# Query projection with the weights held still and rotated along partitions, and one fixed instruction order for a whole two-layer backbone

## The chip, the cores and the metric

The kernel runs on one core of a Trainium2 chip. It is one launch that holds a whole network of two layers. Its time is device microseconds (us), the median of several executions; the profile is of one execution and counts from the first to the last instruction (the span). Engines are named as in the profile: PE (TensorE matmul) with PEld (its weight load), DVE (VectorE), ACT (ScalarE), POOL (GpSimd), and SP, which here only issues transfers. A matmul holds a tile of 128x128 (its "weights") in the array and streams the columns of the other operand past it: "128x512" in a row of the profile is an output of 128 partitions and 512 columns.

## What is computed

Latents `x` (512 tokens x 1024) go through two layers. Each is a token mixer and a dense SwiGLU feed-forward network (FFN), both between RMS norms with shift, scale and gate made from a conditioning vector (`ada`). Layer 0 mixes with windowed grouped-query attention: 16 query heads of 64, 4 key/value heads, a window of 128 tokens to each side, 256 context tokens that every query sees, and a sink logit per head. Layer 1 mixes with a chunked gMLP. Cut to what the change touches:

```
def apply_rope(x, cos, sin):                       # per head of 64: two halves of 32
    x1, x2 = split(x, 2)
    return concat([x1*cos - x2*sin, x2*cos + x1*sin])

def window_sink_mixer(h_lat, h_ctx, w_qkv, w_o, sink, cos, sin):
    q, k, v = split(h_lat @ w_qkv)
    q = apply_rope(q, cos, sin) * 64**-0.5
    k = apply_rope(k, cos, sin)
    ...                                            # softmax over band, context and sink
    return o @ w_o                                 # a plain output projection

def chunk_gmlp(h, ...):
    u, v = split(gelu(h @ w_in + b_in))
    mixed = w_s · layernorm(v) + b_s
    return (u * mixed) @ w_o                       # the other plain output projection
```

## The kernel before

**Arithmetic.** Everything is 32 bits wide. For a full-rate matmul an operand is split into a high part (a cast on ACT, `high`, L217) and a low part, the rest (a subtraction on DVE, `low`, L224); a product is then three matmuls: high by high, high by low, low by high. Weights arrive from memory as `w_raw` in units of 1 MB, and are split into `w_hi` and `w_lo`.

**Stages**, by their time in the profile: norm, modulation and the key/value projection (0 to 78 us); attention (78 to 240); its output projection, called WO (240 to 300); the first FFN (300 to 600), most of it in products of half-size blocks (256 columns), seven in place of eight; the input projections of the gMLP (600 to 716); its output projection, called GO, and the head of the second FFN (716 to 790); the rest of the second FFN (to the end).

**The query path before.** There are 8 pairs `p`, each of four query heads and two tiles of 128 tokens (512 columns in PSUM). `q_project` holds a tile of the activations `HA` still and streams 256 columns of the query weights, 2 tiles x 8 slices x 3 products for a pair, so that the result has tokens on partitions. Then come `q_rows` (ACT copies it out, L736), `rotate` (two multiplications on POOL, L731, and two on DVE, L732, with the table `rope`), `q_add` (DVE, L745), `q_split` (high part on ACT, low part on DVE, L752), `q_turn` (eight PE transposes, L759, since the scores want head dimensions on partitions) and `q_copy` (two ACT copies, L760). A tile `qT` holds in its upper 64 partitions the low part of what the lower 64 hold high, so that a score needs two matmuls, one with `khi` and one with `klo`.

**Attention.** There are 16 blocks, 4 key/value groups x 4 token tiles, with four heads each. A head goes through `score` (PE, L905, into one of two `s_ps` buffers), `bound` (DVE adds the mask and takes the row's bound, L911), `exp` (ACT, L916), `normalise` (POOL, L932), `turn` (PE transposes the probabilities), `turned` (ACT or DVE copy them, L945), `value` (PE), `rows_out` and `store` (L963, L969). Pieces of the query projection of later pairs, of `ada` and of the WO projection stand between these on the same engines.

**What sets the order.** A step is a small function with a due time, `at(time, step, ...)`; `run_plan` (L604) sorts the steps collected so far and calls them. A table of names, `ORDER`, goes before the due times: a step whose name is in it takes its place in the table, and the others follow by time. Inside a "manual schedule" each engine gets its instructions in just the order in which the steps are called; outside one, the framework decides how to interleave them. Before, the table has 1575 names: the start, the attention, and the second half of each plain output projection. The FFNs and the gMLP went by their due times. The first half of each plain output projection (`down`, L1194: units 0 and 1 of four) was not made of steps: loops called `ws.unit`, `ready` (which splits the activations into `st` tiles) and `work` outside a manual schedule. In GO those loops also advanced a generator, `shift_sums` (L1945), which adds up one vector of the second FFN.

An engine works off its instructions in order; one that waits holds up those behind it. The same is true of SP's queue of transfers (`dma`, L214).

## Time and profile before

| | |
|---|---|
| time, median of 3 executions | 1109.83 us (1109.54 to 1112.11) |
| span of the profiled execution | 1108.2 us |
| time less span | 1.6 us |
| PE busy | 1088.3 us, 98% of the span |
| DVE busy | 943.8 us, 85% |
| ACT busy | 612.6 us, 55% |
| POOL busy | 255.9 us, 23% |
| granted PE clock, mean | 0.999 |

The profiled execution has no time of its own beside its span; the 1.6 us are the median less the span. In a row of grouped instructions stand the line, the engine, the operation, what is written from what, the shape, the count, then the busy time and the mean length of one in ns, then the idle time of the engine ahead of them with what ended it. In a row of stretches stand from:to, its length, and the busy time (with the number of instructions) of PE, PEld, DVE, ACT and POOL, then the granted PE clock, the busy share of the DMA engines and GB/s. In a row of waits stand the total, how often, and the longest, in us. Matmuls overlap, and their ends are modelled, so a group's mean length is longer than the pace at which matmuls follow each other; the pace is read from a stretch in which PE is busy throughout.

### The profile page before, as it was taken

The page shows a single profiled execution, that of the slowest core. Times are in us where ns is not written, and L with a number is a line of the kernel's source. Part 1 is how long each engine was busy: PE and PEld are TensorE (multiplying, and loading weights), DVE is VectorE, ACT ScalarE, POOL GpSimd, SP SyncE. Part 2 cuts the span into 40 slices and gives each one's busy share as a digit, 9 for nine tenths or more (in the row PEclk, how much of TensorE's full clock was granted, in tenths as well). Part 3 has the DMA queues.
Part 4 walks back from the last instruction along what each step waited for, and adds up shares of the span by engine and source line. Part 5 has one row for each costly group of instructions (what it writes and reads, how often), then busy time and mean ns, then how long its engine had stood idle before and what let it go on. Part 6 is the DMA issues. An engine that isn't in the chain of part 4 may idle for free.

```text
span 1108.2 us, 17883 instructions
## 1 busy us (share of the span) xinstructions
PE 1088.3 (98%) x6974; PEld 954.9 (86%) x6974; DVE 943.8 (85%) x1418; ACT 612.6 (55%) x1060; POOL 255.9 (23%) x276
## 2 busy tenths in 40 slices
PE   7999999999999999999999999999999999999997
PEld 4788877768799999998888788887999999998876
DVE  5788988958999999987988778878988888879985
ACT  6457767756555545545665534337555545546652
POOL 2517575624600000001321411006400000002300
PEclk9999999999999999999999999999999999999999
DMA  9652333243245655449964286652233343369821
GB/s 366 266 182 86 136 96 115 77 135 113 109 143 172 224 159 185 171 141 330 225 122 128 68 323 241 205 194 77 70 133 124 132 152 126 126 222 319 158 40 76
DMA packets 48857, 179.15 MB, mean 162 GB/s; under 512 B 4859, under 2 KB 9211, under 8 KB 37637
## 3 DMA queue, kind: packets, MB, share of 16 engines
q1 hardware_dynamic: 41220, 163.34, 42.3%
q0 software_dynamic: 7552, 14.68, 7.9%
q8 instruction: 54, 0.88, 0.3%
q14 instruction: 31, 0.25, 0.1%
HBM read 171.71 MB, written 2.10 MB: 157 GB/s over the span
## 4 chain that ended last, share of the span: by engine, by line
PE 64%; DVE 6%; POOL 2%; issue 2%; ACT 1%; DMA 1%; POOLq 0%; DVEq 0%; SPq 0%; ACTq 0%
PE f L1449 35%; PE y L1633 13%; PE y L1660 4%; PE v L281 4%; PE y L281 2%; PE u L1869 1%; PE u L1867 1%; PE u L1868 1%; POOL tmp L1166 1%; DVE w_lo L224 1%; DVE tmp L1170 1%; DVE x L1154 1%; PE mix L1882 1%; DMA w_raw<-in_w 1%; DVE a_sum L1378 1%
## 5 line engine op out<-in xcount | busy, mean ns | idle before, releaser
L1449 PE MATMUL f<-H,w_hi 128*128 128x256 f32 x960 | 178.6, 284 | 1.1 <-DVE fc L1460 0.5
L1449 PEld LDWEIGHTS f<-H,w_hi 128*128 128x128 f32 x960 | 149.7, 192 | 2.3 <-DVE fc L1460 1.4
L1449 PE MATMUL f<-H,w_lo 128*128 128x256 f32 x480 | 135.8, 283 | 0.0
L1633 PE MATMUL y<-w_hi,s 128*128 128x512 f32 x448 | 120.1, 389 | 0.0
L1449 PE MATMUL f<-S,w_hi 128*128 128x256 f32 x640 | 118.6, 283 | 0.0
L217 ACT CAST w_hi<-w_raw 128x1024 fp32r<-128x1024 f32 x90 | 94.5, 1053 | 39.9 <-PE y L1633 8.9
L217 ACT CAST w_hi<-T 128x1024 fp32r<-128x1024 f32 x80 | 83.7, 1047 | 52.4 <-PE f L1449 33.7
L1456 ACT COPY fc<-f 128x256 f32<-128x256 f32 x120 | 44.6, 372 | 105.8 <-PE f L1449 102.7
L224 DVE TENSOR_TENSOR w_lo<-w_raw,w_hi 128x1024 fp32r<-128x1024 f32 (+1 forms) x81 | 96.3, 1193 | 6.7 <-ACT w_hi L217 6.7
L1449 PEld LDWEIGHTS f<-S,w_hi 128*128 128x128 f32 x640 | 99.9, 192 | 0.0
L1633 PEld LDWEIGHTS y<-w_hi,s 128*128 128x128 f32 x448 | 84.1, 188 | 17.5
L224 DVE TENSOR_TENSOR w_lo<-T,w_hi 128x1024 fp32r<-128x1024 f32 x80 | 97.3, 1216 | 0.0
L1449 PEld LDWEIGHTS f<-H,w_lo 128*128 128x128 f32 x480 | 92.1, 192 | 0.0
L1449 PE MATMUL f<-S,w_lo 128*128 128x256 f32 x320 | 90.7, 284 | 0.5 <-DVE w_lo L224 0.5
L1621 POOL DMA_DIRECT2D t<-in_w x48 | 42.2, 929 | 186.5 <-PE y L1660 88.4
L383 DVE SCALAR_TENSOR_TENSOR acc<-ada_k,sc,acc 128x1024 f32<-128x1024 f32 x56 | 71.6, 1278 | 10.3 <-DMA ada_k<-in_ada 8.4
L397 POOL DMA_DIRECT2D acc<-acc x8 | 6.9, 866 | 314.2 <-DVE acc L383 310.4
L1633 PE MATMUL y<-w_lo,s 128*128 128x512 f32 x224 | 69.1, 390 | 0.6 <-DVE w_lo L224 0.6
L1449 PE MATMUL f<-H,x 128*128 128x256 f32 x480 | 64.3, 283 | 0.0
L932 POOL TENSOR_SCALAR p<-p,st 128x512 f32<-128x512 f32 (+1 forms) x64 | 53.4, 849 | 44.4 <-DVE st L928 11.7
L281 PE MATMUL y<-w_hi,st 128*128 128x512 f32 x224 | 62.3, 391 | 0.0
L1449 PEld LDWEIGHTS f<-S,w_lo 128*128 128x128 f32 x320 | 61.4, 192 | 0.9 <-DVE w_lo L224 0.9
(255 smaller groups left out, 2851.6 us busy)
## 6 DMA issues: line engine op xcount, KB each, us to landing
w_raw<-in_w SPq DMA_DIRECT2D x67, 1024.0 KB, 5.0
ada_k<-in_ada SPq DMA_DIRECT2D x56, 512.0 KB, 5.2
ada_raw<-in_ada SPq DMA_DIRECT2D x12, 1024.0 KB, 4.8
w<-in_w SPq DMA_DIRECT2D x12, 1024.0 KB
t<-in_w POOLq DMA_DIRECT2D x48, 256.0 KB, 6.1
ada<-in_ada SPq DMA_DIRECT2D x8, 1024.0 KB, 11.2
t<-in_w SPq DMA_DIRECT2D x8, 1024.0 KB, 9.2
w_raw<-in_w SPq DMA_DIRECT2D x10, 512.0 KB, 5.6
```

The costliest lines, as they stand in the source:

```text
L217: nc.scalar.copy(out=hi, in_=src)
L224: (eng or nc.vector).tensor_tensor(out=v(lo), in0=v(src), in1=v(hi).bitcast(F32), op=ALU.subtract)
L281: nc.tensor.matmul(dst, l, w[:, n * 512:(n + 1) * 512], start=first and i == 0, stop=last and i == 2)
L383: nc.vector.scalar_tensor_tensor(out=self.acc, in0=self.raws.pop(k), scalar=sc[:, k:k + 1], in1=self.acc, op0=ALU.mult, op1=ALU.add)
L932: nc.gpsimd.tensor_scalar(out=p, in0=p, scalar1=self.st[:, 12 + j:13 + j], scalar2=1.0, op0=ALU.mult, op1=ALU.mult)
L1154: nc.vector.scalar_tensor_tensor(out=xt, in0=self.tmp[:, c0:c1], scalar=self.r, in1=xt, op0=ALU.mult, op1=ALU.add)
L1166: nc.gpsimd.tensor_tensor(out=self.tmp[:, D:], in0=x[:, self.t, :], in1=self.nxt[0], op=ALU.mult)
L1449: nc.tensor.matmul(dst, l[:, w], r[:, k, :], start=first and k == 0 and j == 0, stop=k == 3 and j == 2, skip_group_check=True)
L1456: nc.scalar.copy(out=self.c[n][:, i * 256:(i + 1) * 256], in_=self.ps[n, 1 if i == 1 else 0])
L1621: nc.gpsimd.dma_start(out=self.tt[:, p * D + 512 * i:p * D + 512 * (i + 1)], in_=a["w"][F2[self.layer] + 1 + 2 * p + i][:, c:c + 512], acc ...
L1633: nc.tensor.matmul(self.bank7(i, j), st[:, c:c + P], w[:, z * 512:(z + 1) * 512], start=i == 1 and p == 0 and l == 0 and z == 0, stop=p == ...
L1660: nc.tensor.matmul(self.y[t][n], st[:, x + t * P:x + (t + 1) * P], parts[h][w][:, n * 512:(n + 1) * 512], start=v == 0 and h == 0 and i == ...
```

## The change

**Query path.** `q_project(p, k)` now holds 128 columns of the query weights still and streams all 512 tokens, so a pair is two heads for all tokens, and head dimensions come out on partitions. There are 8 pairs still; a group of four heads needs two of them. Both halves of a head are then 32 partitions apart: `q_swap` exchanges them with four transfers on SP's queue (32 partitions x 2 KB each, within SBUF). `q_rows` copies with the scale, `q_cos` and `q_add` are DVE, `q_sin` is POOL, `q_high` and `q_low` (two each, 64 partitions) write the split result straight into `q_X`. The eight transposes and two copies of a pair are gone. `q_cos` works in place, so it waits for the four transfers. The rotation table is transposed once, by 24 small matmuls (`rope_turn`), into `ropeT`. Some buffers shrink: `p` from 11 to 9, `pt` of the attention and `o_sb` from 2 to 1.

**Order.** The table has 3352 names and covers the whole program; the manual schedule stays open to the end. The first half of both plain output projections is made of steps (`stage_hi`, `stage_lo`, `work`, fetches and splits of weights), as are `shift_sums` and the transfers of `x`. With `parted=True` (GO) the steps collected so far run before the buffers are lent on (`lend_units`). A line of the new table in the attention:

```
-q_step_2_1 q_step_2_2 m4fetch_0 score_0_0 q_step_2_3 bound_0_0 exp_0_0 score_0_1 q_step_2_4 m2fetch_gain score_0_2
...
```

The table itself is left out; what it does is shown by the rows further down. The core of the diff:

```diff
-    def q_project(dst, u, t, k):
-
-        hi, lo = (p[:, (k % 4) * 256:(k % 4 + 1) * 256] for p in ws.halves[u, k // 4])
-        mm3(dst, HA[:, k, t * P:(t + 1) * P], HA[:, KC + k, t * P:(t + 1) * P], hi, lo, k == 0, k == KC - 1)
+    def q_project(p, k):
+
+        c = (k % 4) * 256 + (p % 2) * P
+        hi, lo = (w[:, c:c + P] for w in ws.halves[Q0 + p // 2, k // 4])
+        for i, (w, x) in enumerate(((hi, k), (hi, KC + k), (lo, k))):
+            nc.tensor.matmul(q_ps[p], w, HA[:, x, :], start=k == 0 and i == 0, stop=k == KC - 1 and i == 2)
...
+    def rope_turn(z):
+
+        tables[z] = ps = bankA("rope")
+        n = 32 << z
+        for t in range(NT):
+            for r in range(0, P, n):
+                nc.tensor.matmul(ps[r:r + n, t * P:(t + 1) * P], tables["k"][:, t, 32 * z:32 * z + n], ident,
+                                 start=True, stop=True, tile_position=(0, r))
...
-    def q_split(tmp):
-
-        qs = stage("qs").rearrange("p (h d) -> p h d", h=8)
-        q3 = tmp[:, 0:512].rearrange("p (h d) -> p h d", h=8)
-        nc.scalar.activation(out=qs[:, :, 0:HD], in_=q3, func=AF.Copy, scale=HD ** -0.5)
-        nc.vector.scalar_tensor_tensor(out=qs[:, :, HD:], in0=q3, scalar=HD ** -0.5,
-                                       in1=qs[:, :, 0:HD].bitcast(F32), op0=ALU.mult, op1=ALU.subtract)
-        return qs
-
-    def q_turn(qT, qs, i, bank):
-        ps = bank("qT_ps")[:, 0:512]
-        for h in range(GRP):
-            nc.tensor.transpose(ps[:, h * P:(h + 1) * P], qs[:, i * GRP + h, :].bitcast(F32), ident)
-        return lambda: nc.scalar.copy(out=qT[:, :, i * P:(i + 1) * P], in_=ps.rearrange("p (h s) -> p h s", h=GRP))
...
+    def q_rows(p):
+        q_rot[p] = vec("q_rot")
+        nc.scalar.activation(out=q_rot[p][:, 0:SEQ], in_=q_ps[p], func=AF.Copy, scale=HD ** -0.5)
+
+    def q_swap(p):
+
+        for h in range(4):
+            d = 32 * (h ^ 1)
+            dma(q_rot[p][d:d + 32, SEQ:], q_rot[p][32 * h:32 * h + 32, 0:SEQ])
+
+    def q_cos(p):
+        v = q_rot[p][:, 0:SEQ]
+        nc.vector.tensor_tensor(out=v, in0=v, in1=ropeT[:, 0:SEQ], op=ALU.mult)
+
+    def q_sin(p):
+        v = q_rot[p][:, SEQ:]
+        nc.gpsimd.tensor_tensor(out=v, in0=v, in1=ropeT[:, SEQ:], op=ALU.mult)
+
+    def q_add(p):
+        v = q_rot[p][:, 0:SEQ]
+        nc.vector.tensor_tensor(out=v, in0=v, in1=q_rot[p][:, SEQ:], op=ALU.add)
+
+    def q_high(p, z):
+
+        if z == 0:
+            q_X[p] = att_p.tile([P, 2, SEQ], F32R, name="q_X", tag="q_X", bufs=4)
+        r = slice(z * HD, (z + 1) * HD)
+        high(q_X[p][r, z, :], q_rot[p][r, 0:SEQ])
+
+    def q_low(p, z):
+        r, o = slice(z * HD, (z + 1) * HD), slice((1 - z) * HD, (2 - z) * HD)
+        low(q_X[p][o, z, :], q_X[p][r, z, :], q_rot[p][r, 0:SEQ])
...
-            ws.unit(u0)
-            ready(0)
-            for v in range(nu - 2):
-                for t in range(NT):
-                    work(v, t)
-                ws.unit(u0 + v + 1)
-                ws.fetch(u0 + v + 2)
-                ready(v + 1)
-                run(bg, -(-left // (nu - 2 - v)))
-                left -= -(-left // (nu - 2 - v))
-            ws.unit(end - 1)
-            ready(nu - 1)
...
+                for h in range(2):
+                    if (u0 + v, h) not in ws.halves:
+                        at(b + .4 * h - .9, ws.high, u0 + v, h)
+                        at(b + .4 * h - .8, ws.low, u0 + v, h, nc.vector)
+                    k = 2 * v + h
+                    at(b + .4 * h - 1, stage_hi, k)
+                    at(b + .4 * h - .9, stage_lo, k)
+                if v < nu - 2:
+                    for t in range(NT):
+                        at(b + 3 * t, work, v, t)
+            if bg is not None:
+                bg(B)
+            at(B + 12 * nu - 14, ws.fetch, end)
+            if parted:
+                run_plan()
+                lend_units()
+            else:
+                at(B + 12 * nu, lend_units)
```

Three places show how the new order moves instructions. A row is a line of the kernel, an operation, what it writes from what, the shape, and how many stand in a row. Line numbers after the change are higher by about 200.

**SP's queue from the last weight unit before the attention into its first blocks.** `acc<-acc 64x1024` copies half of an `ada` sum to the other partitions; `row`, `acc<-in_ada_b` and `ada_raw` are loads for `ada`. Before:

```order
L214 DMA rope<-in_rope 128x384
L214 DMA w_raw<-in_w 128x2048
L214 DMA acc<-acc 64x1024
L214 DMA ada_raw<-in_ada 128x2048
L214 DMA row<-in_norm_g 128x1024
L214 DMA acc<-in_ada_b 1x1024
L214 DMA w_raw<-in_w 128x2048
```

After:

```order
L414 DMA w_raw<-in_w 128x2048
L414 DMA mask<-in_mask 128x896
L414 DMA q_rot<-q_rot 32x512 x8
L414 DMA w_raw<-in_w 128x2048
L414 DMA q_rot<-q_rot 32x512 x4
L414 DMA acc<-in_ada_b 1x1024
L414 DMA ada_raw<-in_ada 128x2048
L414 DMA acc<-acc 64x1024
L414 DMA row<-in_norm_g 128x1024
L414 DMA q_rot<-q_rot 32x512 x4
```

The transfers of pairs 0 to 2 follow closely, and those of later pairs stand behind loads and an `acc<-acc` of the same queue; the load of `mask`, which before was issued at 17.58 us, now comes after the last `ada_raw` of the start.

**DVE where the key/value projection ends and the attention begins.** `kr` and `klo` belong to the keys; `klo` must be there before the first scores. Before:

```order
L800 TENSOR_TENSOR kr<-ksrc 128x1024 x2
L224 TENSOR_TENSOR w_lo<-w_raw,w_hi 128x512
L224 TENSOR_TENSOR klo<-kT,khi 128x2x256
L224 TENSOR_TENSOR w_lo<-w_raw,w_hi 128x512
L732 TENSOR_TENSOR qr<-qsb,rope 128x8x32 x2
L224 TENSOR_TENSOR klo<-kT,khi 128x2x256
L745 TENSOR_TENSOR qr<-qr 128x512
L224 TENSOR_TENSOR w_lo<-w_raw,w_hi 128x512 x2
L752 SCALAR_TENSOR_TENSOR qs<-qr,qs 128x8x64
L224 TENSOR_TENSOR klo<-kT,khi 128x2x256 x4
```

After:

```order
L958 TENSOR_TENSOR q_rot<-q_rot,ropeT 128x512
L424 TENSOR_TENSOR w_lo<-w_raw,w_hi 128x512 x2
L966 TENSOR_TENSOR q_rot<-q_rot 128x512
L424 TENSOR_TENSOR w_lo<-w_raw,w_hi 128x512
L1014 TENSOR_TENSOR kr<-ksrc 128x1024
L424 TENSOR_TENSOR q_X<-q_rot,q_X 64x512
L424 TENSOR_TENSOR klo<-kT,khi 128x2x256 x2
L424 TENSOR_TENSOR w_lo<-w_raw,w_hi 128x512
L424 TENSOR_TENSOR klo<-kT,khi 128x2x256 x2
L958 TENSOR_TENSOR q_rot<-q_rot,ropeT 128x512
L424 TENSOR_TENSOR klo<-kT,khi 128x2x256 x2
L966 TENSOR_TENSOR q_rot<-q_rot 128x512
```

The second `q_cos` (L958, pair 1), which waits for its transfers, now stands ahead of the last two `klo`.

**ACT where WO begins and where GO begins.** `st` is the high part of the projection's left operand, and the first matmul of `y` needs one; `y_part` is a copy of a part of WO that was computed during the attention; `uT` is the gelu of the gMLP. WO before:

```order
L945 COPY pt<-pT_ps 128x512 x2
L217 CAST st<-oT_908 128x512 x2
L963 COPY o_sb<-o_ps 64x512
L217 CAST st<-oT_908 128x512
L945 COPY pt<-pT_ps 128x512
L217 CAST st<-oT_908 128x512
L963 COPY o_sb<-o_ps 64x512
L1057 COPY y_part<-q_ps 128x512
```

WO after:

```order
L1147 COPY pt<-pT_ps 128x512
L1165 COPY o_sb<-o_ps 64x512
L1249 COPY y_part<-q_ps 128x512
L417 CAST st<-oT_891 128x512 x3
L622 COPY row<-ada_ps 128x512
L417 CAST st<-oT_891 128x512
```

GO before:

```order
L1876 ACTIVATE uT<-u,bu 128x512
L217 CAST st<-uT 128x512 x2
L1876 ACTIVATE uT<-u,bu 128x512
L217 CAST st<-uT 128x512
L217 CAST w_hi<-w_raw 128x1024 x2
L1876 ACTIVATE uT<-u,bu 128x512
L217 CAST st<-uT 128x512
```

GO after:

```order
L2077 ACTIVATE uT<-u,bu 128x512 x3
L417 CAST w_hi<-w_raw 128x1024 x2
L417 CAST acc_st<-acc 128x1024
L2077 ACTIVATE uT<-u,bu 128x512 x3
L417 CAST st<-uT 128x512 x4
L417 CAST w_hi<-w_raw 128x1024 x2
```

In both projections the `st` casts stood among the last copies of the stage before; now all of them come after the last of these.

709 lines of the change are left out of this document (438 added, 271 removed).

## The prediction

> **What bounds the kernel now.** I read the busy shares first, then each stage by itself, since a share over the whole span mixes stages.
>
> ```profile
> span 1108.2 us, 17883 instructions
> PE 1088.3 (98%) x6974; PEld 954.9 (86%) x6974; DVE 943.8 (85%) x1418; ACT 612.6 (55%) x1060; POOL 255.9 (23%) x276
> ```
>
> ```profile
> 0.00:78.00 78.00, 72.42 (x467) 53.72 (x467) 55.75 (x119) 40.30 (x69) 23.19 (x34) 1.00 0.71 270
> 78.00:240.00 162.00, 159.23 (x1084) 125.97 (x1084) 139.29 (x303) 115.60 (x255) 94.75 (x118) 1.00 0.36 118
> 240.00:300.00 60.00, 59.44 (x281) 48.65 (x280) 48.51 (x67) 36.35 (x61) 33.60 (x25) 1.00 0.25 83
> 300.00:500.00 200.00, 198.38 (x1637) 196.87 (x1636) 193.10 (x265) 105.55 (x181) 3.62 (x4) 1.00 0.53 175
> 500.00:620.00 120.00, 118.74 (x555) 98.51 (x553) 99.59 (x128) 71.09 (x106) 30.02 (x33) 1.00 0.70 187
> 620.00:780.00 160.00, 159.03 (x752) 131.56 (x753) 129.10 (x168) 72.13 (x115) 37.64 (x29) 1.00 0.55 188
> 780.00:1000.00 220.00, 219.95 (x1764) 216.56 (x1763) 192.04 (x268) 115.92 (x197) 9.94 (x7) 1.00 0.41 141
> 1000.00:1108.20 108.20, 101.13 (x445) 83.09 (x443) 86.45 (x110) 55.62 (x82) 23.18 (x28) 0.99 0.58 142
> ```
>
> PE is the bound in every stage, at a granted clock of 1.00. Its idle time, length less busy, is 5.6 + 2.8 + 0.6 + 1.6 + 1.3 + 1.0 + 0.0 + 7.1 = 20 us. Only the first stage and the end have more than 3. So a new order alone has little to win; work taken from PE is worth nearly its length. In the attention (78 to 240) DVE is second, with 139.29 of 162. Who waits for whom there:
>
> ```profile
> DVE s_ps L911 <- PE s_ps L905: 7.7, 14, 2.2
> PEld s_ps L905 <- ACT p L916: 4.5, 8, 0.9
> ```
>
> DVE's bounds wait for PE's scores more than the scores wait for a buffer that `exp` frees. PE leads, but by 20 us of 162.
>
> **PE's work in the query path.** The pace of matmuls comes from stretches in which PE has no gap, one with 256 columns each and one with 512:
>
> ```profile
> 340.00:360.00 20.00, 20.00 (x169) 20.00 (x169) 19.42 (x27) 10.49 (x18) 0.00 (x0) 1.00 0.47 162
> 640.00:660.00 20.00, 20.00 (x90) 16.57 (x89) 14.63 (x17) 7.50 (x10) 1.52 (x1) 1.00 0.95 346
> ```
>
> That is 20/169 = 0.118 us and 20/90 = 0.222 us; in the first PEld is full too, in the second not. The trace's groups for the query path, eight transposes in a row elsewhere, and the nearest row to the new small matmuls:
>
> ```profile
> L273 PE MATMUL q_ps<-w_hi,HA 128*128 128x256 f32 x96 | 29.5, 308 | 0.0
> L759 PE MATMUL qT_ps<-ident,qs 128*128 128x128 f32 x64 | 9.9, 277 | 0.6 <-ACT qT L760 0.3 <-DVE pt L945 0.2
> L526 PE MATMUL rows<-ada,s 128*32 128x256 f32 x128 | 8.4, 384 | 0.0
> 625.41 0.87 PE hT L1177 x8
> ```
>
> L273 and its two sister lines make 8 pairs x 48 = 384 matmuls of 256 columns. They become 192 of 512: 192 x (2 x 0.1183 - 0.2222) = **-2.8 us** (bounds 0, if PEld's lead hides the difference, and -2.8). The 64 transposes fall away, at 0.87/8 = 0.109 us each **-7.0** (the other bound, half of it, -3.5, if they fill gaps of the scores). The 24 matmuls of `rope_turn` cost between 8.4/128 = 0.066 and 0.109 us each, 1.6 to 2.6; I take the middle, **+2.1**. Together **-7.7**.
>
> **What the other engines get.**
>
> ```profile
> L732 DVE TENSOR_TENSOR qr<-qsb,rope x16: 407/418/967, 74.2 to 196.3; 128x256 f32<-128x256 f32 x16
> L731 POOL TENSOR_TENSOR qr<-qsb,rope x16: 726/738/923, 72.2 to 196.9; 128x256 f32<-128x256 f32 x16
> L745 DVE TENSOR_TENSOR qr<-qr x8: 673/684/1006, 75.6 to 200.6; 128x512 f32<-128x512 f32 x8
> L752 DVE SCALAR_TENSOR_TENSOR qs<-qr,qs x8: 684/746/974, 77.4 to 202.2; 128x512 fp32r<-128x512 f32 x8
> L224 DVE TENSOR_TENSOR s<-act,s 128x512 fp32r<-128x512 f32 x56 | 38.4, 685 | 7.3 <-ACT s L217 7.0
> L969 DVE TENSOR_TENSOR oT<-o_ps,o_sb 64x256 f32<-64x256 f32 x32 | 13.3, 416 | 1.7 <-ACT o_sb L963 1.2
> ```
>
> (Three numbers with slashes are the shortest, the median and the longest in ns.) 64 partitions of 256 columns take 0.416 us and 128 take 0.418: columns set the price, so each `q_low`, 64x512, costs a whole 0.685. A pair took DVE 2 x 0.418 + 0.684 + 0.746 = 2.27 us, and takes now `q_cos` 0.684, `q_add` 0.684, two `q_low` 1.37, in all 2.74: **+3.8 us** over 8 pairs. DVE goes from 139.3 to about 143 while the stage would shrink from 162 to about 155. `q_sin` for POOL is the two halves of L731 in one, 1.48 us as before. On ACT two copies and a cast turn into two casts. Since DVE still has 12 us to spare, most of its 3.8 lies beside PE's work. I take **+1.0** for the attention (bounds 0 and 3.8).
>
> **The transfers.** The nearest row to `q_swap` is the copy within SBUF of half an `ada` sum, issued on the same queue:
>
> ```profile
> acc<-acc SPq DMA_DIRECT2D x8, 256.0 KB, 2.9
> L214 SPq DMA_DIRECT2D acc<-acc x8: 467/467/523, 77.3 to 976.0; - x8
> SPq L214 <- DVE acc L375: 36.3, 4, 16.4
> SPq L214 <- DMA acc<-acc: 30.3, 3, 14.8
> SPq L214 <- DVE w_lo L224: 24.7, 2, 24.5
> ```
>
> It is issued in 0.47 us and lands 2.9 us later, so four of 64 KB take 4 x 0.47 + 2.9 = 4.8 us from `q_rows` to `q_cos`, an upper bound where SP is free. In the order DVE has 4 to 9 us of other work between the two (counted by rows like those above), which hides them. Without that cover all 8 pairs would cost up to 4.8 each. The last three rows are SP's own waits from 60 to 240 us: long, and a swap queued behind one comes late. They are the slower rival's. Where the key/value projection passes into attention there is less cover: the second `q_cos` stands ahead of the last two `klo`, and the scores need all `klo`. I take **+1.0** (bounds 0 and 2.5, half a swap's way).
>
> **The two output projections.** These rows are the work around the first matmul of each, GO first:
>
> ```profile
> 708.38 1.13 ACT L217 CAST st<-uT 128x512 fp32r<-128x512 f32 x2
> 715.22 0.39 PE L410 MATMUL ada_ps<-acc_st,ones 128*128 128x512 f32 x1
> 715.46 1.05 PE L1882 MATMUL mix<-ws,v 128*128 128x128 f32 x8
> 716.20 0.68 ACT L1876 ACTIVATE uT<-u,bu 128x512 f32<-128x512 f32 x1
> 716.26 0.71 PE L281 MATMUL y<-w_hi,st 128*128 128x512 f32 x2
> 716.78 0.61 ACT L217 CAST st<-uT 128x512 fp32r<-128x512 f32 x1
> ```
>
> ```profile
> 232.75 0.62 ACT L217 CAST st<-oT 128x512 fp32r<-128x512 f32 x1
> 239.24 0.63 PE L281 MATMUL y<-w_hi,st 128*128 128x512 f32 x2
> 239.44 0.59 ACT L1057 COPY y_part<-q_ps 128x512 f32<-128x512 f32 x1 [0.30 <-PE q_ps L275]
> ```
>
> Before, the first `st` casts of GO (708.38) were 8 us old when `y` began (716.26), and `mix` ran right up to it. After, ACT makes the last gelu (0.68) and only then the first cast (0.61), while PE has one `ada_ps` matmul (0.22 at the pace above) to fill: 0.68 + 0.61 - 0.22 = **+1.1** (bounds 0 and 1.3). WO likewise: a cast was ready 6 us ahead (232.75 against 239.24); after, `y_part` (0.59) and the first cast (0.62) both stand between the last copies of attention and the first `y`: **+1.2** (bounds 0 and 1.2). The third product of each also needs DVE's low part, but four matmuls of 0.22 us cover its 0.69.
>
> **The order of the rest.** In the FFNs the same instructions run in a slightly different order. I looked where each `w_lo` of DVE, the second busiest engine there (193.10 of 200), stands against the product that uses it: with the durations of this trace added up row by row it is at least 6.5 us ahead everywhere, so nothing there gets late, and PE at 219.95 of 220 has nothing to win. At the start, `mask`, 448 KB by its shape, goes behind the weights; at 270 GB/s that is 1.7 us in a stretch where PE idles 5.6. I take **-3.0** for all reordering: 1.0 at the start, and 2.0 of the 13 us idle ahead of the last stage (bounds -9 and +2, since a bad place costs as easily).
>
> **Sum:** 1108.2 - 7.7 + 1.0 + 1.0 + 1.1 + 1.2 - 3.0 = 1101.8 us of span. The median stands 1.6 above the span, so the forecast is **1103.4 us**, and its own range, 1100 to 1107.5, is the bounds of the small terms.
>
> **Rivals.**
> *The order wins more.* If the new order takes back 9 of the idle time in place of 3, the time is 1103.4 - 6 = 1097.4 (1092 to 1100). For: 20 us idle is there to be had, 5.6 of them at the start. Against: 7.1 of it lies in the last stage, which ends with the norm and the stores of the output, and there is nothing for PE to do beside them.
>
> *DVE becomes the bound of the attention.* It has 139 + 4 us of work, and its instructions grow longer beside POOL's:
>
> ```profile
> 109.06 1.68 DVE L732 TENSOR_TENSOR qr<-qsb,rope 128x256 f32<-128x256 f32 x2
> 109.54 1.78 POOL L731 TENSOR_TENSOR qr<-qsb,rope 128x256 f32<-128x256 f32 x2
> ```
>
> Two L732 here take 1.68 in place of 2 x 0.418 = 0.84 while POOL's two take 1.78 in place of 1.48. After the change `q_cos` and `q_sin` are both released by the same transfers and so start together. If one holds up the other wholly, DVE waits 1.48 in each of 8 pairs, 11.8 us, and comes to 139.3 + 3.8 + 11.8 = 155 of the stage's 155: nothing of PE's 7.7 is won, and the time is about 1103.4 + 6 = 1109.4 (1107 to 1112), no change. Against: overlaps of this kind exist before (the longest L732 is 0.967), and DVE has kept up. The Trainium skill, page "SBUF — State Buffer", section "SBUF: two separate sides", says that a DVE instruction with two SBUF inputs and a GpSimd instruction that reads SBUF exclude each other for a whole instruction, whichever starts first. By that rule this rival's full price falls due. The trace agrees in part: DVE's 1.68 is longer by 0.84, less than one whole L731 (0.738) for each of the two.
>
> *The swaps come late (slower).* SP's queue is in order, and it waited 9.1 us on average (36.3 over 4) for `acc` to be read. The swaps of pairs 3 to 7 stand behind `ada` loads, weight loads or `acc<-acc`. Then `q_cos` stops DVE, the bounds stand behind it, the two `s_ps` buffers fill, and PE stops. From a wait of about 4 us on (9 of cover less 4.8) it decides: 9.1 - 4 = 5 us late. Three of the five pairs so are 15 us: 1118.4 (1113 to 1124). For: those waits are real rows. Against: they arose because SP ran far ahead with loads that nobody needed yet, and in the new order a load that stands ahead of a swap may have its buffer free by then.
>
> **How the numbers follow.** Chances: forecast 0.47, more from the order 0.20, DVE bound 0.20, late swaps 0.13. A measurement of this kernel tells about 0.3%, 3.3 us, from no change: below 1106.5 is faster, above 1113.2 slower. Faster takes 0.20 of the second, 0.40 of the forecast's 0.47 and 0.04 of the third: 0.64. Slower is the last and a little of the third: 0.14. The rest, 0.22, is the same. The range that leaves 2 in 10 out reaches from the middle of the second case to the end of the third: 1095 to 1112.
>
> **What would show it.** In the attention PE's busy time falls by about 10 us (2.8 + 7.0) and the stage with it; no row of the query's transposes; swap rows landing in about 3 us; `q_cos` with next to no DVE idle ahead of it. At GO and WO a gap of about 1 us on PE ahead of the first `y`, put down to ACT's `st`. FFN stretches of the same length to 1 us. The forecast is wrong if DVE's idle time ahead of `q_cos` is above 5 us in all, if `q_cos` or `q_sin` has a median twice its price, if an FFN stretch moves by over 2 us, or if the start shrinks by more than 3.

## The result: slower by 2.9%

| | before | after |
|---|---|---|
| time, median (lowest to highest) | 1109.71 us (1109.54 to 1112.11) | 1141.99 us (1139.09 to 1145.82) |
| ratio, with its 95% interval | | 1.0289 (1.0264 to 1.0313) |
| span of the profiled execution | 1108.2 us | 1141.0 us |
| matmuls | 6974 | 6766 |

The forecast was 1103.4 us, and the range ended at 1112. The profile of the changed kernel, first its busy time:

```profile
PE 1093.7 (96%) x6766; PEld 944.6 (83%) x6766; DVE 957.8 (84%) x1418; ACT 608.1 (53%) x1054; POOL 257.1 (23%) x268
```

Then its stages, cut as before up to 620 us and, since everything comes later, a little wider behind that:

```profile
0.00:78.00 78.00, 72.26 (x461) 53.55 (x462) 56.70 (x114) 41.14 (x69) 23.68 (x32) 0.98 0.70 269
78.00:240.00 162.00, 151.34 (x856) 109.89 (x854) 141.97 (x296) 111.10 (x241) 95.85 (x112) 0.98 0.36 110
240.00:300.00 60.00, 58.11 (x272) 45.75 (x272) 48.22 (x67) 36.02 (x61) 28.25 (x22) 1.00 0.38 132
300.00:500.00 200.00, 198.16 (x1606) 195.23 (x1605) 189.74 (x256) 101.90 (x176) 9.59 (x8) 1.00 0.51 169
500.00:620.00 120.00, 113.08 (x541) 95.63 (x540) 96.41 (x125) 66.50 (x95) 21.72 (x25) 0.96 0.69 184
620.00:780.00 160.00, 151.93 (x709) 124.92 (x709) 125.59 (x153) 66.12 (x104) 30.67 (x25) 1.00 0.58 194
780.00:1000.00 220.00, 218.29 (x1690) 210.62 (x1689) 192.80 (x271) 115.08 (x202) 23.72 (x18) 1.00 0.34 116
1000.00:1141.00 141.00, 130.56 (x644) 109.01 (x643) 106.37 (x138) 70.27 (x108) 23.63 (x28) 0.99 0.57 156
```

The matmuls did become fewer, by 208, and PE is busy for longer all the same (1093.7 us, where it was 1088.3). Its granted clock was 0.98, 0.98 and 0.96 in three stages that had 1.00 before. That fits, but how much of the 5.4 us it accounts for was not taken apart. Its idle time, the length less the busy time of each row, was 20 us and is 47.

A stage's ends move, so it is better to take one instruction that both kernels have and to subtract its start in one trace from its start in the other. This table is worked out so; each number is how much later (in us) the changed kernel comes to that place, and in the last column what is added since the row above.

| place | before, at | after: later by | added |
|---|---|---|---|
| last matmul of the keys and values | 69.69 | +1.07 | +1.07 |
| first `value` matmul of attention | 104.66 | +9.92 | +8.85 |
| last `value` matmul | 237.91 | +5.61 | -4.31 |
| first `y` of WO | 239.24 | +6.97 | +1.36 |
| first `f` of the first FFN | 299.67 | +7.42 | +0.45 |
| first of its last products (half blocks) | 517.32 | +9.65 | +2.23 |
| last of these | 595.06 | +16.61 | +6.96 |
| last `y` of the first FFN | 616.18 | +18.17 | +1.56 |
| last `u` of the gMLP | 714.99 | +23.80 | +5.63 |
| last `y` of GO | 763.03 | +25.02 | +1.22 |
| first of the second FFN's last products | 1002.73 | +27.91 | +2.89 |
| last of these | 1079.53 | +32.21 | +4.30 |
| end | 1108.20 | +32.78 | +0.57 |

Three places stand out: the start of attention, the last products of each FFN, and the gMLP. Only one stretch gains anything, the attention behind its first `value`.

**The query path** has about the prices that were put on it (shortest, median and longest in ns):

```profile
L958 DVE TENSOR_TENSOR q_rot<-q_rot,ropeT x8: 679/690/860, 72.8 to 185.4; 128x512 f32<-128x512 f32 x8
L962 POOL TENSOR_TENSOR q_rot<-q_rot,ropeT x8: 1272/1324/1809, 70.5 to 183.2; 128x512 f32<-128x512 f32 x8
q_rot<-q_rot SPq DMA_DIRECT2D x32, 64.0 KB, 2.0
```

**Start of attention**, in the order of time, with the first matmuls of pair 2's product on PE; the brackets hold the idle time ahead of a row and what ended it:

```profile
85.67 1.19 PE L868 MATMUL q_ps<-HA,w_hi 128*128 128x512 f32 x2 [6.46 <-DVE klo L424]
86.66 0.63 PE L868 MATMUL q_ps<-HA,w_lo 128*128 128x512 f32 x1
87.09 1.05 PE L868 MATMUL q_ps<-HA,w_hi 128*128 128x512 f32 x2
87.94 0.63 PE L868 MATMUL q_ps<-HA,w_lo 128*128 128x512 f32 x1
```

The first score, the first `bound` on DVE, and the same `bound` in the kernel before:

```profile
93.26 0.39 PE L1107 MATMUL s_ps<-khi,q_X 128*128 128x512 f32 x1
93.92 0.76 DVE L1113 CUSTOM_DVE_ANT_0 s_ps<-s_ps,mask,nsink 128x512 f32<-128x512 f32 x1 [5.64 <-PE s_ps L1107]
```

```profile
81.86 0.76 DVE L911 CUSTOM_DVE_ANT_0 s_ps<-s_ps,mask,nsink 128x512 f32<-128x512 f32 x1 [0.77 <-PE s_ps L905]
```

Now PE stands still for 6.46 us until DVE has made the last `klo`. Pair 2's product needs no key itself. But its output lies in a PSUM pool (`psR`) that the code opens only where it closes the one (`psA`) with the transposed keys, from which `klo` is made. Then the table puts all 24 matmuls of pair 2 ahead of the first score, and the first of them follow each other at (87.94 - 86.66) / 3 = 0.43 us, twice the 0.222 of full speed: the clock had gone down in the hole (the granted clock from 80 to 90 us was 0.66).

**Last products of the first FFN.** The first row is PE's wait, the next ones what ACT, whom it waits for, was doing, and the last ones POOL's issues of an accumulating load:

```profile
PE y L1836 <- ACT s L417: 6.9, 1, 6.9
```

```profile
573.23 1.04 ACT L417 CAST w_hi<-t 128x1024 fp32r<-128x1024 f32 x1 [8.17 <-DMA t<-in_w]
574.18 0.61 ACT L417 CAST s<-act 128x512 fp32r<-128x512 f32 x1
```

```profile
560.47 0.89 POOL L1824 DMA_DIRECT2D t<-in_w  x1 [1.67 <-issue]
561.75 0.89 POOL L1824 DMA_DIRECT2D t<-in_w  x1 [0.39 <-issue]
```

PE needs the `s` of 574.18, which is cheap and whose input was long there. It stands in ACT's order behind a cast of weights (573.23) that waits 8.17 us for its load. In the new table POOL sends the four loads of this product in the order 2, 3, 0, 1, while ACT casts 0, 1, 2, 3. So ACT waits for the load that was sent third. Each load is two transfers; these two were issued at 560.47 and 561.75 and landed 11 us later, where the median is 6.1. SP had issued two loads of `w_raw`, 1 MB each, from 559.17 on, and the DMA engines were full (a busy share of 0.95 from 560 to 565 us and of 1.06 from 565 to 570). How much of the wait is due to these weights was not tested.

### The profile page after: what moved, and what is told of

It reads as the page before. It is cut to its first block, busy times and chain, and to the rows that moved or that the text cites. A ratio compares the mean times of both kernels' runs of the same rounds, so it can differ in the third digit from the quotient of the medians.

```text
span 1141.0 us, 17629 instructions
## 1 busy us (share of the span) xinstructions
PE 1093.7 (96%) x6766; PEld 944.6 (83%) x6766; DVE 957.8 (84%) x1418; ACT 608.1 (53%) x1054; POOL 257.1 (23%) x268
## 4 chain that ended last, share of the span: by engine, by line
PE 48%; DVE 22%; DMA 12%; issue 8%; ACT 5%; POOL 4%; SPq 0%; DVEq 0%; POOLq 0%; ACTq 0%
PE f L1652 22%; PE y L1836 7%; DVE w_lo L424 4%; DMA w_raw<-in_w 4%; PE y L484 4%; DMA t<-in_w 3%; PE y L1863 3%; DVE acc L586 2%; DMA ada_k<-in_ada 2%; DVE T L1612 2%; PE o_ps L1160 2%; DVE s_ps L1113 2%; PE q_ps L868 2%; ACT w_hi L417 2%; PE pT_ps L1140 2%
## 5 line engine op out<-in xcount | busy, mean ns | idle before, releaser
L1652 PE MATMUL f<-s,w_hi 128*128 128x256 f32 x320 | 60.5, 287 | 1.8 <-ACT fc L1659 1.8
```

The source lines that it names most:

```text
L1652: nc.tensor.matmul(dst, l[:, w], r[:, k, :], start=first and k == 0 and j == 0, stop=k == 3 and j == 2, skip_group_check=True)
```

## The experiments

Each is the changed kernel, the one before, or the latter with the new query path (query_only). Most differ from it only by names moved in the table `ORDER`, and then the lines of their diff are pieces of that table. None leaves work out; `more_dve` and `cover_hole` add work whose result nobody uses. "At the first value" means the lateness of the first `value` matmul against the kernel before, as in the table above.

### Which part costs what

**late_old**: the changed kernel, with the order from the end of attention on as it was (both FFNs, gMLP, second half of GO). A piece of it:

```diff
-work_9_0 work_10_0 wfetch_44 wfetch_45 c0square_y#2 ...
+work_9_1 whigh_43_0 work_9_0 work_10_0 wlow_43_0 ...
```

> The changed kernel, but every step behind the attention's output projection (both FFNs, the gMLP, the second half of GO and the head of the second FFN) goes in the order it had before. By the traces of before and after, the lag of the changed kernel grows by 2.2 + 7.0 + 1.6 us in the first FFN, about 6 in the gMLP, 1 in the head and 1.8 + 4.3 in the second FFN. Theory 'the table of the late stages': these some 22 us go, 1117 to 1122 us. Rival 'it is the manual schedule that stays open, or buffers': the order of names does not matter, 1139 to 1145.

Measured: 1127.6 us (1125.7 to 1130.1), ratio 1.0167 (1.0143 to 1.0191). So 14 us of the 32 come back, where some 22 were expected. 4.8 of what stays arise between the first `f` and the first of the last products. PE waits there once for 4.1 us, and the changed kernel has no such row:

```profile
PE fat L1341 <- DVE silu_a L1332: 4.1, 1, 4.1
```

**ffn_new_order**: the kernel before, with only the two FFNs in the new order.

```diff
+f0part_high_3_2 m5start f0product_2_1 m5fetch_chunk_0_spare f0product_2_5 f0diff_3_1 ...
+f1product_2_1 f1keep_2_0 f1product_2_2 f1gate1_2 m5fetch_chunk_1_spare#2 ...
```

> The kernel before, with nothing changed but the order of the steps of both FFNs, which is that of the changed kernel. Theory 'the table': the 17 us that the two FFNs lost in the changed kernel appear here, 1122 to 1129 us, with PE idle in the seven-product parts while ACT waits for accumulating loads. Rival 'manual schedule or buffers': 1108 to 1112.

Measured: 1133.0 us (1132.2 to 1135.4), ratio 1.0214 (1.0197 to 1.0231). 23 us, with no other part of the change present: +5.0 ahead of the first FFN's last products, +7.7 in them, +3.4 and +7.0 in the second. The same hole is there as in the changed kernel, and ahead of the last products PE waits for DVE, 4.3 us in all, most often for `w_lo`. The two rows are waits in the first FFN:

```profile
PE y L1839 <- ACT s L423: 5.4, 1, 5.4
PE f L1655 <- DVE w_lo L430: 1.8, 2, 1.0
```

**gmlp_new_order**: the kernel before, with only the first FFN's last rows and the gMLP in the new order.

```diff
-m2fetch_chunk_0 m2fetch_chunk_1 wfetch_46 wfetch_47 m2start#2 lend_u0 v_part_0_(2,) ...
+m2fetch_chunk_0 v_part_3_(2,) m2fetch_chunk_3 m2fetch_chunk_2 m2fetch_chunk_1 m2start#2 wfetch_46 ...
```

> The kernel before with the order of the changed kernel in the last rows of the first FFN and the input projections of the gMLP only. Theory 'the table there costs what the changed kernel lost there', 1.6 + 5.6 us: 1115 to 1118. Rival 'that loss came with the state that the earlier stages left': 1109 to 1112.

Measured: 1118.5 us (1116.3 to 1120.4), ratio 1.0086 (1.0068 to 1.0104). 10 us, nearly all of it up to the last `u`. PE's longest wait there:

```profile
PE u L1868 <- DVE w_lo L223: 4.1, 1, 4.1
```

**query_only**: the kernel before, with the new query path and the new order only up to the end of attention.

```diff
-    def q_project(dst, u, t, k):
+    def q_project(p, k):
...
```

> The kernel before with the new query path alone, and the new order up to the end of the attention; everything behind it as before. Theory 'attention itself is slower by the lag of 5.6 us read at its last value matmul': 1113 to 1118 us, with a hole of about 6.5 us on PE at 79 us. Rival 'the query path saves what was forecast and only what is put behind it loses': 1103 to 1108.

Measured: 1114.2 us (1113.8 to 1115.0), ratio 1.0042 (1.0027 to 1.0057). The query path with its order costs 4.5 us, where the prediction had it win. It is 9.7 late at the first value, 6.7 at the last one and 5.0 at the end. The three parts together (4.5, 23 and 10 us) are more than the 32 of the whole; where they overlap wasn't looked into.

**one_o_sb**: the kernel before with the smaller `o_sb`.

```diff
-            self.half = att_p.tile([HD, 512], F32, name="o_sb", tag="o_sb", bufs=2)
+            self.half = att_p.tile([HD, 512], F32, name="o_sb", tag="o_sb", bufs=1)
```

> The kernel before with one buffer in place of two for the copy of the attention's output (o_sb), as in the changed kernel. Theory 'the smaller buffers cost some of the loss in the attention': 1111 to 1114. Rival 'they cost nothing': 1109 to 1110.5.

Measured: 1109.3 us, ratio 1.0004 (0.9995 to 1.0014): nothing. Its order is the old one, and yet its last key matmul came 1.7 us later than in the kernel before, and the stretch from the last `u` to the last `y` of GO was 1.5 us shorter. So 1 or 2 us in these two rows of the table above needn't come from the order. The smaller `p` and `pt` on the old order weren't tried.

### The last products: order of the loads

**tadd_early**: the changed kernel, with each accumulating load as early as its buffer allows, and no eye to the order.

```diff
-f0t7_add_2_22 f0t7_add_0_22 ... f0t7_add_2_11 ... f0t7_add_3_11 f0t7_add_0_11 f0t7_add_1_11 ...
+f0t7_add_1_22 f0t7_add_0_22 f0t7_add_3_22 ... f0t7_add_0_11 ... f0t7_add_1_11 ...
```

> The changed kernel, with only the 24 steps moved that issue the accumulating loads of the seven-product parts on POOL: each stands right behind the step that it depends on. Theory 'in the seven-product parts these loads are issued too close to their use': of the 7.0 + 1.6 + 4.3 us lost there most comes back, 1130 to 1135 us. Rival 'it is the places of the casts on ACT and DVE, whatever the loads do': 1139 to 1144.

Measured: 1141.9 us, ratio 1.0293 (1.0272 to 1.0315): no gain. There is still a hole, earlier, ahead of the product before, with the same form on ACT. The loads are out of step here too, one product earlier: POOL sends 1, 0, 3, 2, and ACT casts 2, 0, 1, 3. The wait of PE, and the cast:

```profile
PE y L1843 <- ACT s L424: 3.1, 1, 3.1
```

```profile
548.30 1.04 ACT L424 CAST w_hi<-t 128x1024 fp32r<-128x1024 f32 x1 [7.34 <-DMA t<-in_w]
```

**adds_matched**: the changed kernel, with the loads in the order in which ACT casts them, and as early as in tadd_early.

```diff
-2_22 0_22 1_22 3_22 2_11 3_11 0_11 1_11 0_21 1_21 3_21 2_21
+2_22 0_22 1_22 3_22 0_11 1_11 2_11 3_11 0_21 2_21 1_21 3_21
```

> The changed kernel (1142.0 us) with the 24 steps moved that issue the accumulating loads in the seven-product parts: POOL issues them in the order in which ACT's casts need them, each as early as what it depends on allows. (In tadd_early each was early, but the order on POOL no longer fitted that of the casts.) Theory 'the table lets POOL serve the loads of slices 2 and 3 ahead of 0 and 1 while ACT casts 0 and 1 first, and what PE needs stands behind that cast': the hole of 7.3 us at 567 us goes and most of the 4.3 us in the second FFN, 1131 to 1136 us. Rival 'the loads come late in any order': 1139 to 1143.

Measured: 1136.8 us (1134.1 to 1138.6), ratio 1.0244 (1.0225 to 1.0263). In the first FFN the last products take 1.8 us less than before the change, where they took 7.0 more. These 8.7 us aren't the order alone, since the loads are also earlier. The clean pair is tadd_early and this kernel. On every engine the computing instructions have the same order, and in the first FFN the loads of product 6 (`11`) stand in the same places in step; what differs is the order of the first four loads (`22`), and that two of the last four (`21`) have changed places. The last products take 5.0 us more than before the change in the one and 1.8 less in the other, so 6.8 us are the order. ACT's waits for these loads between 500 and 620 us, in the kernel before, the changed one and this one:

```profile
ACT w_hi L217 <- DMA t<-in_w: 4.9, 3, 2.5
```

```profile
ACT w_hi L417 <- DMA t<-in_w: 13.8, 5, 8.2
```

```profile
ACT w_hi L424 <- DMA t<-in_w: 4.7, 4, 1.5
```

In the second FFN they still lose 6.6 us, more than the changed kernel's 4.3, though the loads are in step here too; so their order doesn't account for that loss. There ACT waits for a load again, and the DMA engines are full (the row's busy share of 1.07), with PE waiting behind it:

```profile
1030.00:1045.00 15.00, 11.78 (x40) 9.20 (x39) 8.62 (x10) 5.89 (x8) 4.27 (x6) 0.78 1.07 276
```

```profile
PE y L1843 <- ACT r L1851: 3.2, 1, 3.2
```

**adds_crossed**: the kernel before, with nothing moved but these loads. In both FFNs the four of product 6 go together to where the last of them stood; in the first network out of step, in the second in step.

```diff
 f0: ... product7_7_2
+2_11 3_11 0_11 1_11   (were 0_11 1_11 2_11 3_11, one behind each block)
 f1: ... product7_7_2
+0_11 1_11 2_11 3_11
```

> The kernel before, with only the accumulating loads of the last products moved on POOL's queue. In both feed-forward networks the four loads that complete the weights of product 6 are issued together, behind the third matmul block of product 7, so all of them later than before. In the first network their order is 2, 3, 0, 1 while ACT casts 0, 1, 2, 3; in the second it is 0, 1, 2, 3. Theory (the order of the loads against the order of the casts makes the hole): in the first network PE gets a hole of 3 to 7 us behind ACT's casts and the stretch of the last products takes 3 to 8 us longer; in the second at most 2 us. In all 1112 to 1119 us. Rival (lateness alone makes it): both networks lose alike. Rival (the hole of the changed kernel came from the order of products and casts, which stays as it was here): neither loses more than 1 us, 1109 to 1111.

Measured: 1111.6 us (1110.0 to 1115.1), ratio 1.0021 (1.0009 to 1.0033). The first FFN's last products take 2.4 us longer, the second's not a hundredth. So the crossing costs and the lateness alone doesn't, but the price is below the 3 to 8 expected. ACT waits nearly as long as in the changed kernel (12.6 us for 13.8), and PE only 1.2:

```profile
ACT w_hi L422 <- DMA t<-in_w: 12.6, 5, 6.0
PE y L1838 <- ACT r L1846: 1.2, 1, 1.2
```

In the old order less stands behind the waiting cast: it has `w_hi` of product 6 behind the second block of product 3, the new one ahead of the first. That fits a hole that needs both, a load out of step and casts of `s` queued behind it; the casts alone weren't moved. The control ran in the other network, where the surroundings differ.

### The gMLP

**brow_early**: gmlp_new_order, with one load moved on SP.

```diff
-wfetch_47 m2fetch_chunk_4 m2add_chunk_1 ... m4fetch_chunk_1 row_in_0 ws_in
+wfetch_47 row_in_0 m2fetch_chunk_4 m2add_chunk_1 ... m4fetch_chunk_1 ws_in
```

> The kernel before with the changed order of the first network's last rows and of the gMLP (that kernel took 1118.5 us), and in it the load of the first bias row (512 KB, broadcast) moved on SP's queue from behind seven loads of ada to ahead of them, about 18 us earlier. Theory (DVE stands 5.3 us behind this load, its layer norms come late and pile up ahead of the last w_lo of u, for which PE waits 4.1 us): the wait of 5.3 goes, the 4.1 us hole of PE shrinks to under 1.5, and the time falls by 3 to 5 us, to 1113.5 to 1115.5. Rival (the hole is there because w_lo stands at its late place in DVE's order, whatever DVE waited for before): the wait goes, the hole stays above 3 us, 1117 to 1119.

Measured: 1119.5 us (1117.9 to 1120.0), ratio 1.0086 (1.0066 to 1.0106): no gain. DVE's wait for this load is gone, but one of 5.1 us for `ada_k` came in its place, and PE's hole only fell from 4.1 to 3.4. DVE's rows ahead of it show what the late `w_lo` stands behind; its high part was cast at 685.55:

```profile
685.74 1.27 DVE L1852 SCALAR_TENSOR_TENSOR vtmp<-vtmp,mu,row 128x1024 f32<-128x1024 f32 x1
687.46 1.28 DVE L1856 SCALAR_TENSOR_TENSOR v<-vtmp,rv,row 128x1024 f32<-128x1024 f32 x1 [0.44 <-POOL rv L253]
688.66 1.28 DVE L1852 SCALAR_TENSOR_TENSOR vtmp<-vtmp,mu,row 128x1024 f32<-128x1024 f32 x1
689.86 1.28 DVE L382 SCALAR_TENSOR_TENSOR acc<-ada_k,sc,acc 128x1024 f32<-128x1024 f32 x1
691.05 1.28 DVE L1834 TENSOR_TENSOR vtmp<-v,brow 128x512 f32<-128x512 f32 x2
692.25 1.21 DVE L223 TENSOR_TENSOR w_lo<-w_raw,w_hi 128x1024 fp32r<-128x1024 f32 x1
```

From 685.74 on DVE has no idle time but 0.44 us. Five steps of about 1.2 us stand ahead of `w_lo`, and none of them is needed by PE then. That fits the rival, the place of `w_lo` in DVE's order. It isn't settled, since the long wait changed its cause and didn't go; moving `w_lo` alone wasn't tried.

### The start of attention and its inside

**keys_first**: query_only, with the steps of the keys ahead of those of the queries.

```diff
-k_copy_2 k_rope_2 k_add_2 q_first_1_4 q_first_1_5 q_rows_0 q_swap_0 q_sin_0 whigh_3_0 ... k_split_0_0 q_sin_1
+k_copy_0 k_copy_2 table_Exp k_rope_2 k_add_2 k_rope_0 k_add_0 ... k_split_4_0 k_split_4_1 q_first_1_4 ... q_add_0
```

> The kernel of query_only (1114.2 us), with the steps between the key/value projection and the first scores in another order: the projection of pair 0 behind that of the keys, the whole chain of the keys (rotation, transposes, split) ahead of the query's on DVE and ACT, and the projection of pair 1 between the transposes of the keys. Theory 'the hole of 7.4 us on PE at 78 us comes from the chain of klo, which starts late and stands behind query and weight work on DVE': the first value matmul comes 4 to 6 us earlier, 1108 to 1110.5 us. Rival 'the attention behind it is bound by DVE alone, and what is gained ahead is waited for later': 1113 to 1115.

Measured: 1113.9 us, ratio 1.0038 (1.0026 to 1.0051). The last `klo` is made at 80.2, and the first `bound` still comes at 93.05. PE now waits 3.3 us in pair 2's product for the low part of its weights, the rest of the 24 matmuls follows, and on DVE the last steps of pair 1 come right up to the `bound`:

```profile
PE q_ps L660 <- DVE w_lo L214: 3.3, 1, 3.3
```

**pair1_later**: pair 1's rotation behind the first scores, half of pair 2's projection too. **start3**: pair 1 early, half of pair 2's projection behind the first scores.

```diff
-q_step_2_0 ... q_step_2_7 q_rows_2 ... block_0 score_0_0 ...
+q_step_2_0 ... q_step_2_3 block_0 score_0_0 score_0_1 q_step_2_4 ... q_step_2_7 bound_0_0 ...
 pair1_later, behind these:
+q_cos_1 q_sin_1 q_add_1 q_high_1_0 q_low_1_0 q_high_1_1 q_low_1_1
```

> The kernel of query_only (1114.2 us) with another order at the start of the attention: the keys' chain first on DVE, the weight split of pair 2 in its gaps, the scores and bounds of the first two heads of blocks 0 and 1 ahead of the finish of pair 1 (rotation, split). In keys_first PE's hole was only moved and the first bound stayed at 93.1 us. Theory 'the attention is bound by DVE, so its length is set by how early DVE gets to the bounds': the first bound comes 5 us or more earlier (86 to 88) and the time with it, 1108 to 1110.5 us. Rival 'DVE then waits later for pair 1 or for scores': 1112 to 1115.

> The kernel of query_only (1114.2 us) with the start of the attention in a third order, mended where pair1_later waited: the keys' chain first on DVE, q_rows of pair 1 ahead of the casts of pair 0 on ACT, q_rows of pair 2 ahead of the casts of pair 1, the first two scores ahead of half of pair 2's projection, the other two behind three steps of pair 3's. Theory 'what the start loses is carried to the end, and it is lost to the order in which ACT, DVE and PE take the long query path': the first value matmul comes 3 to 5 us earlier than in query_only and the time falls by as much, 1109 to 1111.5. Rival 'the way itself is too long, whatever the order': the first value matmul comes less than 1 us earlier, 1113 to 1115.

Measured: 1114.4 us, ratio 1.0043 (1.0031 to 1.0056), and 1115.7 us, ratio 1.0066 (1.0053 to 1.008). Both bring the first `bound` 9 us forward, and both pay for it at the next place. The first two rows are of pair1_later, the others of start3:

```profile
84.89 0.76 DVE L906 CUSTOM_DVE_ANT_0 s_ps<-s_ps,mask,nsink 128x512 f32<-128x512 f32 x1 [0.75 <-issue]
93.75 1.22 PE L660 MATMUL q_ps<-HA,w_hi 128*128 128x512 f32 x2 [4.61 <-ACT q_rot L740]
```

```profile
84.23 0.76 DVE L906 CUSTOM_DVE_ANT_0 s_ps<-s_ps,mask,nsink 128x512 f32<-128x512 f32 x1
102.08 1.22 DVE L758 TENSOR_TENSOR q_rot<-q_rot 128x512 f32<-128x512 f32 x1 [6.16 <-POOL q_rot L754]
```

At the first value they are 9.0 and 10.9 us late, where query_only is 9.7.

**queries_early**: query_only, with both first pairs projected ahead of the last context matmuls.

```diff
-kv_5_5 ... kv_7_5 ... q_first_1_0
+q_first_0_0 ... q_first_0_7 kv_5_5 q_first_1_0 q_first_1_1 kv_6_4 ... kv_7_5
```

> The kernel of query_only (1114.2 us) with the projections of pairs 0 and 1 both ahead of the context's last key/value products, so that their exchange of halves and rotation run under PE's work on the context and the keys' transposes; the keys' chain and the weight split of pair 2 in between. Theory 'the start of the attention waits for the long way of the new query path, some 10 us from q_rows to the first scores, which had no other work beside it': the first value matmul comes 5 us earlier than in query_only (9.7 us later than before) and the time falls to 1108.5 to 1111. Rival 'what is won there is waited for behind it': the lag at the last value matmul stays above 5.5 us, 1113 to 1115.

Measured: 1119.0 us, ratio 1.0089 (1.0074 to 1.0105): the last key matmul comes 5.6 us later, the first value 13.9. What goes ahead of the keys makes the keys late.

**cover_hole**: query_only, with 30 matmuls of no use in the hole.

```diff
+    def cover():
+        ps = bankA("cover")
+        for i in range(30):
+            nc.tensor.matmul(ps, HA[:, 0, 0:P], HA[:, 0, :], start=True, stop=True)
```

> The kernel of query_only with 30 matmuls of 128x512 on data at hand (results unused, 6.7 us) put into the hole on PE between the transposes of the keys and pair 2. Nothing that anyone waits for changes. Theory 'after the hole PE runs at a lower clock for some us (the 24 matmuls behind it take 7.6 us in place of 5.3)': the lower clock goes and 2 us are won, 1111.5 to 1112.5. Rival 'that clock does not hang on the hole, or what it costs is hidden': 1113.5 to 1115.

Measured: 1113.1 us, ratio 1.0035 (1.0021 to 1.0048). That is 1.1 us less than query_only, and the intervals overlap, so the time alone doesn't show a gain; neither expected range holds it. The same 10 us in query_only and here:

```profile
80.00:90.00 10.00, 4.01 (x11) 3.24 (x12) 7.19 (x10) 2.89 (x5) 2.19 (x2) 0.66 0.48 147
```

```profile
80.00:90.00 10.00, 9.90 (x44) 7.89 (x43) 6.71 (x10) 2.90 (x5) 2.22 (x2) 1.00 0.52 143
```

The granted clock goes from 0.66 to 1.00 and the first value comes 2.0 us sooner. So about 2 of the 9.7 go with the clock, by one trace of each kernel.

**more_dve** and **turned_act**: query_only with one more multiplication on DVE for six pairs, and with eight copies moved from DVE to ACT. **add_on_pool**: `q_add` of six pairs on POOL. **both**: turned_act with pair1_later.

```diff
 more_dve:
+        if p > 1:
+            nc.vector.tensor_tensor(out=q_rot[p][:, SEQ:], in0=v, in1=ropeT[:, 0:SEQ], op=ALU.mult)
 add_on_pool:
-        nc.vector.tensor_tensor(out=v, in0=v, in1=q_rot[p][:, SEQ:], op=ALU.add)
+        (nc.gpsimd if p > 1 else nc.vector).tensor_tensor(out=v, in0=v, in1=q_rot[p][:, SEQ:], op=ALU.add)
 turned_act:
-            (nc.vector.tensor_copy if i % 2 else nc.scalar.copy)(out=pt, in_=self.ps[i])
+            dve = i % 2 and not (i == 3 and self.t in (1, 2))
+            (nc.vector.tensor_copy if dve else nc.scalar.copy)(out=pt, in_=self.ps[i])
```

> The kernel of query_only with one more DVE multiplication of 128x512 (0.69 us, its result unused) for each of pairs 2 to 7: 4.1 us more for DVE. Theory 'DVE is the bound of the attention': 3 to 4.5 us slower, 1117 to 1118.7. Rival 'PE is, DVE has room': within 1 us of 1114.2.

> The kernel of query_only with 8 of the 32 copies of transposed probabilities that DVE makes (0.68 us each, 5.4 us in all) given to ACT, in the same places of the order. Theory 'DVE bounds the attention, by its work': 3 to 5 us faster, 1109.5 to 1111.5. Rival 'what DVE gives up, the exponentials behind the copies on ACT lose': 1113 to 1116.

> The kernel of query_only with q_add of pairs 2 to 7 on POOL in place of DVE: 6 x 0.69 = 4.1 us less for DVE, some 8 us more for POOL. Theory 'DVE is the bound of the attention' (18.9 to 19.5 of 20 us busy from 100 to 220): 3 to 4 us faster, 1110 to 1111.5. Rival 'PE is': 1113.5 to 1115, or slower if the longer way through POOL makes q_X late.

> pair1_later and turned_act together. If both theories hold they add, 5 + 4 us: 1104 to 1107 us, faster than the kernel before (1109.7). If the second limit behind DVE is PE, less: 1107 to 1110. If neither holds: 1112 to 1116.

Measured: more_dve 1120.0 us, ratio 1.0093 (1.008 to 1.0107); turned_act 1114.9, 1.0049 (1.0037 to 1.0062); add_on_pool 1115.1, 1.0049 (1.0037 to 1.0062); both 1114.2, 1.0044 (1.003 to 1.0057). Against query_only's 1114.2, six multiplications on DVE (6 x 0.69 = 4.1 us) cost 5.8 us, and taking work from DVE wins nothing. From 100 to 220 us, the kernel before and then query_only; behind these the waits around the scores (from 100 to 246 us), first query_only's and then turned_act's:

```profile
100.00:220.00 120.00, 119.20 (x820) 93.54 (x819) 108.02 (x238) 87.14 (x195) 77.26 (x96) 1.00 0.32 105
```

```profile
100.00:220.00 120.00, 116.09 (x674) 84.22 (x673) 114.61 (x245) 90.45 (x198) 80.42 (x96) 1.00 0.36 115
```

```profile
PEld s_ps L899 <- ACT p L910: 6.6, 13, 0.9
DVE s_ps L905 <- PE s_ps L899: 2.3, 6, 0.6
```

```profile
PEld s_ps L899 <- ACT p L910: 7.8, 15, 1.1
DVE s_ps L905 <- PE s_ps L899: 4.6, 10, 0.7
```

PE's lead over DVE has shrunk from 119.2 - 108.0 = 11.2 us to 116.1 - 114.6 = 1.5. With less to do, DVE waits longer for the scores (4.6 us for 2.3), and the scores longer for ACT's `exp` (7.8 for 6.6). That fits three engines that go round in one loop through the two `s_ps` buffers, so that relief for one leaves the time to the other two; no run singles this out.

No kernel here is faster than the one before.

## Why the prediction was wrong

Its terms against the table above, in us of span:

| step | predicted | measured |
|---|---|---|
| start | -1.0 | +1.1 |
| passage into attention | +1.0 (0 to 2.5) | +8.9 |
| rest of attention (-7.7 for PE, +1.0 for DVE) | -6.7 | -4.3 |
| WO | +1.2 | +1.4 |
| GO | +1.1 | +1.2 |
| the order of the rest | -2.0 | +24.6 |
| sum | -6.4 | +32.8 |

The first three rows don't compare as they stand, because the -7.7 isn't all in the third. `rope_turn` (+2.1) runs at the start, and four pairs in place of three are projected between the start and the first `value`. A pair costs 48 x 0.1183 = 5.7 us before and 24 x 0.2222 = 5.3 after. With the prediction's own prices put where the work lies, the start was to be 0.8 longer, the passage 3.6 longer and the rest 10.9 shorter.

**The order of the rest** is the step that failed. It said that `w_lo` is "at least 6.5 us ahead everywhere, so nothing there gets late", and set +2 as the worst. Three things are wrong with it. It added up durations on DVE and compared them with PE, but left out the loads and ACT: the 6.9 us hole is an ACT cast waiting for a load on POOL's queue with PE's operand behind it. It let no engine wait; the changed kernel has PE waiting for `w_lo` in the second FFN's last products, and so has ffn_new_order in the first FFN, both found safe, and in the gMLP, which the sum didn't go through, PE waits 4.1 us. The changed kernel's rows:

```profile
PE y L1836 <- DVE w_lo L424: 2.3, 3, 1.5
PE u L2070 <- DVE w_lo L424: 4.1, 2, 2.5
```

And its bound of +2, "since a bad place costs as easily", had no row behind it, while the new table holds some 1800 names more than the old (3352 less 1575). The order of the loads accounts for the first FFN's last products: 6.8 us between tadd_early and adds_matched, where the changed kernel lost 7.0. For the second FFN's last products and the gMLP these waits are on record, and ffn_new_order and gmlp_new_order show that the new order of these stages alone brings the loss; what makes `w_lo` late in it stays open.

**The start** came out near its price of +0.8; kernels with the same start came to the last key matmul 0.2 to 1.1 us late, and one_o_sb with the old start 1.7.

**The passage into attention** was named as the place with little cover, and sized at half a swap's way. Of the 8.9 us, 2.6 are work that has moved here from the rest of attention (the added pair less the transposes), and 5.3 weren't priced. The swaps were on time (2.0 us). What was missed is the chain: the keys' steps stand behind the queries' on DVE, PE idles 6.5 us for `klo`, its clock falls, and 24 matmuls stand ahead of the first score. keys_first, pair1_later, start3 and queries_early each take away one link, and the next one then holds at nearly the same time. Whether a better order exists for the longer query path, or its length alone sets the price, stays open.

**Rest of attention.** The 208 fewer matmuls and the absence of transposes are as said, and PE's busy time does fall. The gain is 4.3 in place of 10.9. DVE's added work, hidden by "12 us to spare" in the prediction, fits that: from 100 to 220 us PE has a lead of 1.5 us left in query_only, and more_dve shows that further work on DVE costs its length. Yet relief for DVE won nothing, so DVE alone isn't what holds the stage. So the rival in which DVE becomes the bound was half right, by its 3.8 us of work and not by its lock. That lock was hardly put to the test: in five of the eight pairs `q_sin` was over before `q_cos` began, and in the others they overlapped by 0.65 us at most (there `q_cos` took 0.693 and `q_sin` 1.809). The medians of `q_cos` and `q_sin` are 0.690 and 1.324, near or below their prices. By the rule of the Trainium skill's page "SBUF — State Buffer", section "SBUF: two separate sides", two such instructions exclude each other for a whole instruction; with so little overlap this trace can't settle it.

**Late swaps**, the slower rival, did not come: DVE had no idle time ahead of any `q_cos`. Its side was right in sign for a reason that no rival had. **WO and GO** have the waits for ACT's late casts as worked out, about 1 us each. That the whole stretch at GO is 1.2 longer, as forecast, is partly luck: PE waits another 1.6 there for DVE's low part, which the prediction had as covered, and the rest of the stretch, which was 1.5 shorter in one_o_sb too, made up for it. The rows at GO:

```profile
PE y L484 <- DVE st L424: 1.6, 1, 1.6
PE y L484 <- ACT st L417: 1.1, 1, 1.1
```

Of the signs named ahead, "an FFN stretch moves by over 2 us" is the one that showed it, by nearly 11 us in the first.
